# Inverting the chunked recurrence on packed 64x64 blocks instead of full 128x128 matrices

## The chip, the cores and the metric

The kernel runs on one core of one Trainium2 chip. The time is the device time of one execution in microseconds, from the first to the last instruction of the core; the table below gives the median of three runs. One further execution was profiled, and all rows come from that one.

## What is computed

The program computes two transformer blocks on 256 tokens of width 1024. The first has four mixers side by side (a chunked linear recurrence, a spatial gate, a short convolution, a diagonal state-space scan), a merge and a squared-ReLU network; the second has two kinds of attention and a product-key expert layer. Only the recurrence is touched:

```python
def step(state, inp):
    r_t, w_t, k_t, v_t, a_t, b_t = inp
    sa = jnp.einsum('bhij,bhj->bhi', state, a_t)
    state = (state * w_t[:, :, None, :] + sa[..., None] * b_t[:, :, None, :]
             + v_t[..., None] * k_t[:, :, None, :])
    return state, jnp.einsum('bhij,bhj->bhi', state, r_t)
```

It has four heads of 64 channels. The kernel cuts the 256 tokens into two chunks of 128. Within a chunk the steps depend on each other through a strictly triangular 128x128 matrix M for each head (token s acts on token t > s), and the recurrence is solved by multiplying with X = (I - M)^-1, up to the sign that the code folds into M. That is eight inverses of 128x128: four heads, two chunks.

## The kernel before

Weights stream from HBM in units of 128x1024. Each is split into a high and a low part (`unit`, lines 197 to 210): ScalarE makes the high part (204), VectorE and, in the stage looked at here, GpSimd for two of eight slices make the low part (207, 209). TensorE multiplies three times per tile (`mm3`, 227 to 231: high by high, high by low, low by high). Three raw buffers are shared with `ada_steps` (412), whose VectorE steps at 422 and 424 add up the conditioning vectors, with one-column products at 428.

Around this dense stream other parts run as generators (`spawn`, `tick`): `wkv` is the recurrence, `s5_main` the state-space scan, `sg` the spatial gate. Each `yield` gives control back to the dense stream, so the recurrence's steps are laid between the dense products. The framework's scheduler then orders each engine's queue; each queue runs in order. All PSUM tiles of the generators share the name `ax` and six banks.

The inversion is at lines 801 to 836. It doubles the size of the inverted diagonal blocks seven times. Level l takes the part of M that couples neighbouring blocks of 2^l (`mm`, a product with the constant 0/1 mask `lev[:, l]` on GpSimd, 814), and with X the inverse so far and Z its transpose computes `t1 = mm^T Z` (817), copies it to SBUF (`ts`, ScalarE, 823), and adds `ts^T X` to X (830, 836) and `X^T ts` to Z (834, 835). Index n is the chunk; the four heads lie in one tile of 128x4x128 = 512 elements a partition. Level 0 starts from the identity (819, 820), and level 6 needs no new Z. TensorE operands here are full float32. The names `kn`, `s3` hold the masked matrices of the two chunks, `s2`, `s1` their Z, `bt`, `kt` their `ts`; in the rows `s` stands for several of these (numbers are left out).

Line 784 multiplies halves of 64 rows, with the two row halves going to two PSUM tiles. Lines 864 and 865 have 64 output columns, and the two column halves go to one PSUM tile. Lines 1020, 1042 and 1043 are the state-space products on 32 rows or 32 columns.

Of the kernel before, what the change touches and what calls it, by code (L numbers as in the profile page):

```python
# [8 lines left out]
FT = mybir.dt.float32  # L9
# [4 lines left out]
AF = mybir.ActivationFunctionType  # L14
OP = mybir.AluOpType
# [3 lines left out]
P = 128  # L19
# [47 lines left out]
def _constants():  # L67
    f = np.float32
    r = np.arange(P)
    s, t = r[:, None], r[None, :]  # L70
    ident = np.eye(P, dtype=f)
    ones = np.ones((P, P), f)
    bones = ((s // 64) == (t // 64)).astype(f)
    strict = (s < t).astype(f)
    incl = (s <= t).astype(f)
    iota = np.broadcast_to(r.astype(f)[None, :], (P, P))
    rot = np.zeros((P, P), f)
    for h in (0, 64):
        for i in range(8):
            rot[h + i, h + i + 8] = -1.0  # L80
            rot[h + i + 8, h + i] = 1.0
    main = np.concatenate([ident, ones, iota, bones, strict, incl], axis=1)
    lv = []
    for l in range(7):
        b = 1 << l
        lv.append(((s // (2 * b) == t // (2 * b)) & (s % (2 * b) < b) & (t % (2 * b) >= b)).astype(f))
    levels = np.concatenate(lv, axis=1)
    inv = np.power(f(500000.0), -np.arange(8, dtype=f) / f(8)).astype(f)
    ang = (np.arange(S, dtype=f)[:, None] * inv[None, :]).astype(f)
    cos, sin = np.cos(ang).astype(f).T, np.sin(ang).astype(f).T  # L90
    ct, st = np.ones((P, S), f), np.zeros((P, S), f)
    for h in (0, 8, 64, 72):
        ct[h:h + 8], st[h:h + 8] = cos, sin
    tri = np.where(t <= s, f(0), f(-NEG))
    amask = np.concatenate([tri, np.zeros((P, P), f), tri], axis=1)
    sel = np.zeros((P, 8, S), f)
    for h in range(8):
        sel[h::32, h] = 1.0
    att = np.concatenate([rot.T, ct, st, amask, sel.reshape(P, -1)], axis=1).astype(f)
    return main.astype(f), levels.astype(f), att  # L100


def _layout(inputs):
    a = {k: np.asarray(v) for k, v in inputs.items()}
    one = lambda n: a[n][0]
    m = {}
    m["vec"] = _pack_vectors(a)
    m["main"], m["levels"], m["att"] = _constants()
    m["x"] = a["x"].reshape(S, D).T.reshape(8, P, S).transpose(1, 0, 2)
    m["ada"] = one("ada_w").reshape(8, P, 6, D).transpose(2, 0, 1, 3)[2:]  # L110
# [50 lines left out]
class Kernel:  # L161
# [511 lines left out]
    def wkv(self, psum, pw, pA, y):  # L673
        nc, tc = self.nc, self.tc
        V, SC, G, T = nc.vector, nc.scalar, nc.gpsimd, nc.tensor
        def tl(name, shape=(P, 2, S), dt=FT, **kw):
            return pw.tile(list(shape), dt, name=name, **kw)

        lev = tl("lev", [P, 7, P])
        nc.sync.dma_start(lev, self.A["levels"].rearrange("p (a b) -> p a b", a=7))  # L680
        lw = tl("lw", [P, 256])
        nc.sync.dma_start(lw, self.A["lora"])
# [38 lines left out]
        a = tl("s3")  # L721
# [27 lines left out]
        kn = tl("kn")  # L749
# [16 lines left out]
        bt, kt = (tl(n, [P, 4, P]).rearrange("p (c n) t -> p c (n t)", c=2) for n in ("bt", "kt"))  # L766
# [10 lines left out]
        for n in range(2):  # L777
            yield
            for src, dst in ((bt, mb[n]), (kt, mk[n])):
                for par in range(2):  # L780
                    R = slice(64 * par, 64 * par + 64)
# [16 lines left out]
        bk = tl("bk", [P, 2, 2, P])  # L798
        SC.activation(bk, tps, AF.Copy)
        yield  # L800
        X, Z = {}, {}
        idb = self.ident[:, None, :].to_broadcast([P, 4, P])

        def mt4(n):
            return mb[n].rearrange("p a c (x t) -> p (a c) x t", x=2)[:, :, 0, :]

        for n in range(2):
            X[n], Z[n] = tl(f"X{n}", [P, 4, P]), tl(f"s{2 - n}", [P, 4, P])
        for l in range(7):
            mm, t1, ts = {}, {}, {}  # L810
            yield
            for n in range(2):
                mm[n] = tl(("kn", "s3")[n], [P, 4, P])
                G.tensor_tensor(mm[n], mt4(n), lev[:, l:l + 1, :].to_broadcast([P, 4, P]), op=OP.mult)
                t1[n] = psum.tile([P, 4, P], FT, name="ax")
                for h in range(4):
                    T.matmul(t1[n][:, h, :], mm[n][:, h, :], self.ident if l == 0 else Z[n][:, h, :], start=True, stop=True)
                if l == 0:
                    V.tensor_tensor(X[n], mm[n], idb, op=OP.add)
                    V.tensor_tensor(Z[n], t1[n], idb, op=OP.add)  # L820
                else:
                    ts[n] = tl(("bt", "kt")[n], [P, 4, P])
                    SC.activation(ts[n], t1[n], AF.Copy)
            if l == 0:
                continue
            yield
            for n in range(2):
                xp = psum.tile([P, 4, P], FT, name="ax")
                for h in range(4):
                    T.matmul(xp[:, h, :], ts[n][:, h, :], X[n][:, h, :], start=True, stop=True)  # L830
                if l < 6:
                    zps = psum.tile([P, 4, P], FT, name="ax")
                    for h in range(4):
                        T.matmul(zps[:, h, :], X[n][:, h, :], ts[n][:, h, :], start=True, stop=True)
                    V.tensor_tensor(Z[n], Z[n], zps, op=OP.add)
                V.tensor_tensor(X[n], X[n], xp, op=OP.add)
        O = tl("s4", [P, 2, 2, 2, 64])
        st = tl("st", [P, 2, 64])
        for n in range(2):
# [4 lines left out]
            for par in range(2):  # L844
                R = slice(64 * par, 64 * par + 64)
# [13 lines left out]
            if n == 0:  # L859
                sp = psum.tile([P, 2, 64], FT, name="ax")  # L860
                for c in range(2):
                    for par in range(2):
                        R = slice(64 * par, 64 * par + 64)
# [5 lines left out]
            for par in range(2):  # L869
                R = slice(64 * par, 64 * par + 64)  # L870
                op = psum.tile([P, 2, 64], FT, name="ax")
# [24 lines left out]
        of, kq, kn = tl("s3"), tl("s1"), tl("kn")  # L896
# [730 lines left out]
```

## Time and profile before

| what | us |
|---|---|
| median of 3 runs (1606.66 to 1611.36) | 1610.3 |
| the profiled execution | 1612.27 |
| its span | 1610.5 |
| TensorE products busy | 1555.3 |
| VectorE busy | 1141.2 |
| ScalarE busy | 840.0 |
| GpSimd busy | 367.3 |
| mean granted TensorE clock | 0.985 |

PE is TensorE's products, PEld its weight loads, DVE VectorE, ACT ScalarE, POOL GpSimd. Products are pipelined: the time between two starts tells their rate, and the duration of one is longer than that. The clock is told as a share of 2.4 GHz; 0.50 is 1.2 GHz.

### The profile page before, as it was taken

Reading aid. Unit: us, or ns where it says so; the run is one execution under the profiler, and the core shown is the slowest. Engines: PE = TensorE matmul, PEld = TensorE weight load, DVE = VectorE, ACT = ScalarE, POOL = GpSimd, SP = SyncE. Lnnn points to the kernel's source line nnn. Section 1 sums busy time; section 2 is a strip of 40 time slices with the busy share of each in tenths; the row PEclk is TensorE's granted clock in tenths of the full one; section 3 lists DMA queues with packets and bytes.
Section 4 is the critical chain, followed back from the end, with each engine's and each line's share of the span. In section 5 each row is a group of like instructions: output and inputs, shape, how many; then the busy total and the mean of one; then the engine's idle time right before and its main releaser. Section 6 shows DMA issues by size and latency. Waiting matters only on the chain. (4 is left out here: it accounts for less than half of the span.)

```text
span 1610.5 us, 28420 instructions
## 1 busy us (share of the span) xinstructions
PE 1555.3 (97%) x11206; PEld 1444.6 (90%) x11206; DVE 1141.2 (71%) x1800; ACT 840.0 (52%) x1393; POOL 367.3 (23%) x319
## 2 busy tenths in 40 slices
PE   7998999999999989999999999999999999999997
PEld 5897889999999978989999999999999788888886
DVE  7689876688656676557679887888899555555555
ACT  4562223556644445545354547777776445444443
POOL 7516753416500020003784510000000000000000
PEclk9899899999999999999999999999999999999999
DMA  8555446576665643445655565544445666666663
GB/s 333 181 154 156 132 148 191 176 221 223 176 192 177 204 132 118 131 118 165 214 157 176 180 184 149 153 145 145 148 144 155 190 205 185 193 194 195 193 193 125
DMA packets 75446, 279.87 MB, mean 174 GB/s; under 512 B 8368, under 2 KB 8880, under 8 KB 73648
## 3 DMA queue, kind: packets, MB, share of 16 engines
q1 hardware_dynamic: 75312, 278.05, 56.4%
q8 instruction: 88, 1.44, 0.4%
q14 instruction: 46, 0.38, 0.1%
HBM read 275.92 MB, written 2.10 MB: 173 GB/s over the span
## 5 line engine op out<-in xcount | busy, mean ns | idle before, releaser
L204 ACT ACTIVATE whi<-raw 128x1024 fp32r<-128x1024 f32 x453 | 479.0, 1058 | 582.7 <-PE mm L230 240.2
L207 DVE TENSOR_TENSOR wlo<-raw,whi 128x1024 fp32r<-128x1024 f32 (+2 forms) x413 | 501.5, 1216 | 266.5 <-ACT whi L204 265.3
L229 PE MATMUL mm<-hh,whi 128*128 128x256 f32 x1816 | 525.1, 289 | 1.2 <-ACT uD L464 1.2
L231 PE MATMUL mm<-hh,wlo 128*128 128x256 f32 x1816 | 516.8, 285 | 6.0 <-DVE wlo L207 5.2
L230 PE MATMUL mm<-hl,whi 128*128 128x256 f32 x1816 | 513.3, 283 | 1.1 <-DVE hl L1450 0.7
L231 PEld LDWEIGHTS mm<-hh,wlo 128*128 128x128 f32 x1816 | 346.3, 191 | 8.9 <-DVE wlo L207 6.2
L229 PEld LDWEIGHTS mm<-hh,whi 128*128 128x128 f32 x1816 | 345.3, 190 | 9.2 <-issue 7.4
L230 PEld LDWEIGHTS mm<-hl,whi 128*128 128x128 f32 x1816 | 346.5, 191 | 2.9 <-issue 1.4
L209 POOL TENSOR_TENSOR wlo<-raw,whi 128x256 fp32r<-128x256 f32 (+2 forms) x112 | 185.8, 1664 | 138.9 <-ACT whi L204 85.9
L1484 PE MATMUL ax<-whi,ah 128*128 128x512 f32 x512 | 158.7, 391 | 3.9 <-ACT ah L330 3.9
L1484 PE MATMUL ax<-whi,al 128*128 128x512 f32 x512 | 158.5, 391 | 0.0
L1484 PE MATMUL ax<-wlo,ah 128*128 128x512 f32 x512 | 158.0, 390 | 0.0
L1484 PEld LDWEIGHTS ax<-whi,ah 128*128 128x128 f32 x512 | 96.0, 188 | 23.8 <-ACT ah L330 4.1
L1484 PEld LDWEIGHTS ax<-whi,al 128*128 128x128 f32 x512 | 96.5, 189 | 20.5 <-DVE al L331 0.4
L1484 PEld LDWEIGHTS ax<-wlo,ah 128*128 128x128 f32 x512 | 96.4, 188 | 20.1
L1408 ACT ACTIVATE om<-xres,tg 128x128 f32<-128x128 f32 x256 | 84.9, 392 | 1.0 <-DVE xres L1405 1.0
L231 PE MATMUL ax<-hh,wlo 128*128 128x258 f32 x256 | 72.8, 284 | 1.5 <-DVE wlo L207 1.5
L229 PE MATMUL mm<-fh,whi 128*128 128x256 f32 x256 | 73.0, 285 | 0.0
L231 PE MATMUL mm<-fh,wlo 128*128 128x256 f32 x256 | 72.9, 285 | 0.0
L230 PE MATMUL mm<-fl,whi 128*128 128x256 f32 x256 | 72.9, 285 | 0.0
L229 PE MATMUL ax<-hh,whi 128*128 128x258 f32 x256 | 72.7, 284 | 0.0
L230 PE MATMUL ax<-hl,whi 128*128 128x258 f32 x256 | 72.2, 282 | 0.0
(526 smaller groups left out, 2486.1 us busy)
## 6 DMA issues: line engine op xcount, KB each, us to landing
raw<-in_wts SPq DMA_DIRECT2D x453, 512.0 KB, 3.7
raw<-in_ada SPq DMA_DIRECT2D x24, 512.0 KB, 3.8
araw<-in_ada SPq DMA_DIRECT2D x8, 1024.0 KB, 7.9
w0r<-in_w SPq DMA_DIRECT2D x8, 576.0 KB, 8.9
araw<-in_ada SPq DMA_DIRECT2D x8, 512.0 KB, 4.9
x<-in_x SPq DMA_DIRECT2D x1, 1024.0 KB, 5.3
mb<-in_x SPq DMA_DIRECT2D x2, 512.0 KB, 5.5
selh<-in_att SPq DMA_DIRECT2D x1, 1024.0 KB, 7.2
```

The lines of the kernel that those rows point to most:

```text
L204: nc.scalar.activation(hi, raw, AF.Copy)
L207: nc.vector.tensor_tensor(lo[:, :c], raw[:, :c], hi[:, :c].bitcast(FT), op=OP.subtract)
L209: nc.gpsimd.tensor_tensor(lo[:, c:], raw[:, c:], hi[:, c:].bitcast(FT), op=OP.subtract)
L229: mm(ps, wh, xh, start=start, stop=False, **kw)
L230: mm(ps, wh, xl, start=False, stop=False, **kw)
L231: mm(ps, wl, xh, start=False, stop=stop, **kw)
L1408: SC.activation(om[:, j, :], oe[:, j, :], AF.Copy, scale=it["g"][:, t0 + j:t0 + j + 1])
L1484: T.matmul(acc[t][c], a[:, u, z], w[:, c * 512:(c + 1) * 512], start=i + u == 0 and n == 0, stop=i + u == P - 1 and n == 2)
```

## The change

Levels 0 to 5 never couple the two 64-token halves of a chunk. So the change works on the two diagonal 64x64 blocks alone, packed: tokens 0 to 63 on partitions 0 to 63 and tokens 64 to 127 on partitions 64 to 127, with 64 columns each. X, Z, the masked matrices and `t1` then have 256 elements a partition instead of 512, and each product of 128x128 by 128 becomes two of 64x64 by 64, one on the upper row and column half of the array and one on the lower. `mp` is the packed copy of M (four ScalarE copies of 64 partitions), `Xp` the packed X; `lev` holds six masks of 64 columns and an identity. The masks of level l + 1 are issued in front of level l's second step. The last level writes its result into the diagonal blocks of the full X, which GpSimd has filled with zeros before. The seventh level is one coupling: the off-diagonal 64x64 block of M times the two inverses, in two steps, without masks, written to X by ScalarE.

```diff
-    for l in range(7):
+    s6, t6 = s % 64, t[:, :64]
+    for l in range(6):
...
-        lev = tl("lev", [P, 7, P])
+        lev = tl("lev", [P, 7, 64])
...
+        def masked(l):
+            for n in range(2):
+                mm[n] = tl(("kn", "s3")[n], [P, 4, P])[:, 0:2, :].rearrange("p a (b t) -> p (a b) t", b=2)
+                G.tensor_tensor(mm[n], mp[n], lev[:, l:l + 1, :].to_broadcast([P, 4, 64]), op=OP.mult)
+
         for n in range(2):
-            X[n], Z[n] = tl(f"X{n}", [P, 4, P]), tl(f"s{2 - n}", [P, 4, P])
-        for l in range(7):
-            mm, t1, ts = {}, {}, {}
+            X[n] = tl(f"X{n}", [P, 4, P])
+            G.memset(X[n], 0.0)
...
+            for R in halves:
+                SC.activation(mp[n][R], mt4(n)[R, :, R], AF.Copy)
+        masked(0)
+        for l in range(6):
...
-                    T.matmul(t1[n][:, h, :], mm[n][:, h, :], self.ident if l == 0 else Z[n][:, h, :], start=True, stop=True)
+                    for R in halves:
+                        T.matmul(t1[n][R, h, :], mm[n][R, h, :], lev[R, 6, :] if l == 0 else Z[n][R, h, :], start=True, stop=True)
...
+            if l < 5:
+                masked(l + 1)
...
-                    T.matmul(xp[:, h, :], ts[n][:, h, :], X[n][:, h, :], start=True, stop=True)
...
+                    for R in halves:
+                        T.matmul(xp[R, h, :], ts[n][R, h, :], Xp[n][R, h, :], start=True, stop=True)
+                zps = psum.tile([P, 4, 64], FT, name="ax")
+                for h in range(4):
+                    for R in halves:
+                        T.matmul(zps[R, h, :], Xp[n][R, h, :], ts[n][R, h, :], start=True, stop=True)
+                V.tensor_tensor(Z[n], Z[n], zps, op=OP.add)
+                if l < 5:
+                    V.tensor_tensor(Xp[n], Xp[n], xp, op=OP.add)
+                else:
+                    for R in halves:
+                        V.tensor_tensor(X[n][R, :, R], Xp[n][R], xp[R], op=OP.add)
+        yield
+        for n in range(2):
...
+                T.matmul(t1[n][up_, h, :], mt4(n)[lo, h, up_], Z[n][lo, h, :], start=True, stop=True)
...
+            SC.activation(ts[n][up_], t1[n][up_], AF.Copy)
+        yield
+        for n in range(2):
...
+                T.matmul(xp[lo, h, :], ts[n][up_, h, :], X[n][up_, h, up_], start=True, stop=True)
+            SC.activation(X[n][lo, :, up_], xp[lo], AF.Copy)
```

The scheduler lays TensorE's queue as it was: each group of products stands between the same neighbours. On VectorE the order of neighbours shifts in places. This is VectorE's queue at the updates of level 4, before (`acc` is the conditioning sum at 424, `wlo` a low part, `t1`, `t2` and `sc` the state-space scan, `s2` and `s1` the two Z):

```order
L424 SCALAR_TENSOR_TENSOR acc_1963<-raw_2409,ca_106,acc_1963 128x1024
L1030 SCALAR_TENSOR_TENSOR sc_2280<-s5m_82,z_2275 128x256 x2
L1032 TENSOR_TENSOR t1_2283<-sc_2280,s5t_81 128x512
L1033 TENSOR_TENSOR t2_2284<-sc_2280,s5t_81 128x512
L207 TENSOR_TENSOR wlo_2355<-raw_2352,whi_2354 128x768
L207 TENSOR_TENSOR wlo_2416<-raw_2413,whi_2415 128x768
L424 SCALAR_TENSOR_TENSOR acc_1963<-raw_2489,ca_106,acc_1963 128x1024
L835 TENSOR_TENSOR s2_1727<-s2_1727,ax_2390 128x512
L836 TENSOR_TENSOR X0_1726<-X0_1726,ax_2385 128x512
L835 TENSOR_TENSOR s1_1729<-s1_1729,ax_2402 128x512
L836 TENSOR_TENSOR X1_1728<-X1_1728,ax_2397 128x512
```

And the same place of the changed kernel, whose lines 852 and 854 are the two updates, 426 the conditioning sum and 209 the low part:

```order
L1064 SCALAR_TENSOR_TENSOR sc_2374<-s5m_82,z_2369 128x256 x2
L426 SCALAR_TENSOR_TENSOR acc_2009<-raw_2527,ca_106,acc_2009 128x1024
L1066 TENSOR_TENSOR t1_2377<-sc_2374,s5t_81 128x512
L1067 TENSOR_TENSOR t2_2378<-sc_2374,s5t_81 128x512
L209 TENSOR_TENSOR wlo_2457<-raw_2454,whi_2456 128x768
L209 TENSOR_TENSOR wlo_2534<-raw_2531,whi_2533 128x768
L852 TENSOR_TENSOR s2_1730<-s2_1730,ax_2496 128x256
L854 TENSOR_TENSOR Xp0_1728<-Xp0_1728,ax_2487 128x256
L852 TENSOR_TENSOR s1_1737<-s1_1737,ax_2516 128x256
L854 TENSOR_TENSOR Xp1_1735<-Xp1_1735,ax_2507 128x256
L426 SCALAR_TENSOR_TENSOR acc_2009<-raw_2611,ca_106,acc_2009 128x1024
```

The conditioning sum that stood right ahead of the four updates (`raw_2489`, now `raw_2611`) stands behind them. The second place is GpSimd's queue around the masks of level 1, before (`xx` and `z` belong to the state-space scan):

```order
L1035 TENSOR_TENSOR xx_1690<-t1_1686,t2_1687 128x256
L1036 TENSOR_TENSOR xx_1690<-t1_1686,t2_1687 128x256
L209 TENSOR_TENSOR wlo_1751<-raw_1748,whi_1750 128x256
L814 TENSOR_TENSOR kn_1854<-mb0_888,lev_884 128x512
L814 TENSOR_TENSOR s3_1863<-mb1_892,lev_884 128x512
L209 TENSOR_TENSOR wlo_1825<-raw_1822,whi_1824 128x256
L1025 TENSOR_TENSOR z_1804<-t1_1802,t2_1803 128x256
L1026 TENSOR_TENSOR z_1804<-t1_1802,t2_1803 128x256
```

And the same place of the changed kernel:

```order
L1069 TENSOR_TENSOR xx_1690<-t1_1686,t2_1687 128x256
L1070 TENSOR_TENSOR xx_1690<-t1_1686,t2_1687 128x256
L211 TENSOR_TENSOR wlo_1765<-raw_1762,whi_1764 128x256
L814 TENSOR_TENSOR kn_1815<-mp0_1729,lev_884 128x256
L814 TENSOR_TENSOR s3_1817<-mp1_1736,lev_884 128x256
L211 TENSOR_TENSOR wlo_1847<-raw_1844,whi_1846 128x256
L1059 TENSOR_TENSOR z_1826<-t1_1824,t2_1825 128x256
L1060 TENSOR_TENSOR z_1826<-t1_1824,t2_1825 128x256
```

The masks keep their place, though the code issues them earlier; they are half as large and read the packed copy. TensorE's queue at the updates of level 1, before, with the low-part product ahead of it and the state-space products behind:

```order
L231 MATMUL mm_1875<-hh_70,wlo_1751 128x256
L830 MATMUL ax_1907<-X0_1726,bt_1861 128x128 x4
L834 MATMUL ax_1912<-bt_1861,X0_1726 128x128 x4
L830 MATMUL ax_1919<-X1_1728,kt_1870 128x128 x4
L834 MATMUL ax_1924<-kt_1870,X1_1728 128x128 x4
L1042 MATMUL ax_1670<-xx_1690,s5c_80 32x256
```

And now:

```order
L233 MATMUL mm_1905<-hh_70,wlo_1765 128x256
L847 MATMUL ax_1937<-Xp0_1728,bt_1885 64x64 x8
L851 MATMUL ax_1946<-bt_1885,Xp0_1728 64x64 x8
L847 MATMUL ax_1957<-Xp1_1735,kt_1896 64x64 x8
L851 MATMUL ax_1966<-kt_1896,Xp1_1735 64x64 x8
L1076 MATMUL ax_1670<-xx_1690,s5c_80 32x256
```

The neighbours are the same, and each row of four products has become one of eight smaller ones.

## Rows read from the trace of the kernel before

**Rows 1.** The page: engine sums (us, share, instructions), and TensorE's clock in 40 slices.

```profile
PE 1555.3 (97%) x11206; PEld 1444.6 (90%) x11206; DVE 1141.2 (71%) x1800; ACT 840.0 (52%) x1393; POOL 367.3 (23%) x319
...
PEclk9899899999999999999999999999999999999999
```

**Rows 2.** Stretches: busy time of each engine, granted clock, DMA.

```profile
core 0: us, PE busy (x) PEld busy (x) DVE busy (x) ACT busy (x) POOL busy (x), PEclk, DMA share, GB/s
150.00:200.00 50.00, 45.44 (x305) 40.17 (x305) 43.47 (x51) 13.81 (x18) 36.48 (x31) 0.90 0.45 133
200.00:260.00 60.00, 56.48 (x446) 52.81 (x447) 44.71 (x53) 16.71 (x22) 30.86 (x25) 0.97 0.52 159
260.00:300.00 40.00, 39.16 (x313) 37.68 (x312) 22.25 (x30) 17.05 (x34) 16.29 (x14) 0.96 0.66 210
161.20:164.60 3.40, 3.20 (x15) 2.90 (x14) 0.88 (x2) 0.84 (x2) 3.40 (x4) 0.50 0.57 193
174.90:181.60 6.70, 6.70 (x33) 6.70 (x33) 6.08 (x10) 0.16 (x1) 2.67 (x3) 0.50 0.57 164
232.90:236.20 3.30, 3.23 (x12) 2.32 (x12) 2.03 (x3) 1.19 (x2) 2.06 (x2) 0.50 0.29 115
292.40:296.10 3.70, 3.70 (x26) 3.19 (x24) 0.74 (x1) 0.66 (x2) 1.32 (x1) 1.00 0.37 87
```

**Rows 3.** Waits, 140 to 262: who for whom, total us, times, longest.

```profile
ACT whi L204 <- PE mm L230: 44.1, 11, 7.3
...
PE ax L817 <- DVE s L835: 4.2, 2, 3.3
...
PE ax L817 <- POOL kn L814: 3.1, 1, 3.1
```

**Rows 4.** TensorE in order of time (start, us, instruction), level 1 updates.

```profile
167.57 1.05 PE L830 MATMUL ax<-X,bt 128*128 128x128 f32 x8
168.46 1.06 PE L834 MATMUL ax<-bt,X 128*128 128x128 f32 x8
```

**Rows 5.** TensorE in order of time at the column halves.

```profile
268.49 0.28 PE L230 MATMUL mm<-hl,whi 128*128 128x256 f32 x1
268.61 0.28 PE L231 MATMUL mm<-hh,wlo 128*128 128x256 f32 x1
268.82 0.34 PE L864 MATMUL ax<-us,bk 128*64 128x64 f32 x4
268.99 0.29 PE L865 MATMUL ax<-vt,bk 128*64 128x64 f32 x4
269.10 0.33 PE L864 MATMUL ax<-us,bk 128*64 128x64 f32 x4
269.22 0.34 PE L865 MATMUL ax<-vt,bk 128*64 128x64 f32 x4
269.49 0.38 PE L229 MATMUL mm<-yh,whi 128*128 128x256 f32 x1
```

**Rows 6.** TensorE in order of time at the row halves.

```profile
119.25 1.14 PE L784 MATMUL ax<-ar,bt 64*128 64x256 f32 x8
120.22 1.13 PE L784 MATMUL ax<-ar,kt 64*128 64x256 f32 x8
```

**Rows 7.** GpSimd in order of time before the level 1 products.

```profile
158.57 2.29 POOL L814 TENSOR_TENSOR kn<-mb,lev 128x512 f32<-128x512 f32 x1
160.82 2.09 POOL L814 TENSOR_TENSOR s<-mb,lev 128x512 f32<-128x512 f32 x1
```

**Rows 8.** VectorE in order of time at the level 4 updates.

```profile
229.79 1.28 DVE L424 SCALAR_TENSOR_TENSOR acc<-raw,ca,acc 128x1024 f32<-128x1024 f32 x1 [2.95 <-DMA raw<-in_ada]
230.99 0.68 DVE L835 TENSOR_TENSOR s<-s,ax 128x512 f32<-128x512 f32 x1
```

**Rows 9.** TensorE in order of time behind the level 1 updates.

```profile
173.69 2.56 PE L428 MATMUL ax<-main,acc 128*128 128x1 f32 x16 [0.35 <-DVE s L835]
```

**Rows 10.** VectorE groups, 140 to 262: count, busy us, mean ns, idle before.

```profile
L835 DVE TENSOR_TENSOR s<-s,ax 128x512 f32<-128x512 f32 x10 | 6.8, 678 | 1.7 <-PE ax L834 1.7
...
L430 DVE TENSOR_TENSOR mod<-ax,vec 128x8 f32<-128x8 f32 x2 | 0.3, 162 | 0.4 <-PE ax L428 0.4
```

More of the change, by code (lines that the diff above doesn't have):

```diff
@@ L83, in _constants @@
     lv = []
-    for l in range(7):
+    s6, t6 = s % 64, t[:, :64]
+    for l in range(6):
         b = 1 << l
-        lv.append(((s // (2 * b) == t // (2 * b)) & (s % (2 * b) < b) & (t % (2 * b) >= b)).astype(f))
+        lv.append(((s6 // (2 * b) == t6 // (2 * b)) & (s6 % (2 * b) < b) & (t6 % (2 * b) >= b)).astype(f))
+    lv.append((s6 == t6).astype(f))
     levels = np.concatenate(lv, axis=1)
@@ L800, in wkv @@
         yield
-        X, Z = {}, {}
-        idb = self.ident[:, None, :].to_broadcast([P, 4, P])
+        X, Xp, Z, mp, mm = {}, {}, {}, {}, {}
+        idp = lev[:, 6:7, :].to_broadcast([P, 4, 64])
+        lo, up_ = slice(0, 64), slice(64, 128)
+        halves = (lo, up_)
         def mt4(n):
             return mb[n].rearrange("p a c (x t) -> p (a c) x t", x=2)[:, :, 0, :]
+        def masked(l):
+            for n in range(2):
+                mm[n] = tl(("kn", "s3")[n], [P, 4, P])[:, 0:2, :].rearrange("p a (b t) -> p (a b) t", b=2)
+                G.tensor_tensor(mm[n], mp[n], lev[:, l:l + 1, :].to_broadcast([P, 4, 64]), op=OP.mult)
@@ L807, in wkv @@
         for n in range(2):
-            X[n], Z[n] = tl(f"X{n}", [P, 4, P]), tl(f"s{2 - n}", [P, 4, P])
-        for l in range(7):
-            mm, t1, ts = {}, {}, {}
+            X[n] = tl(f"X{n}", [P, 4, P])
+            G.memset(X[n], 0.0)
+            Xp[n], mp[n] = tl(f"Xp{n}", [P, 4, 64]), tl(f"mp{n}", [P, 4, 64])
+            Z[n] = tl(f"s{2 - n}", [P, 4, P])[:, 0:2, :].rearrange("p a (b t) -> p (a b) t", b=2)
+            for R in halves:
+                SC.activation(mp[n][R], mt4(n)[R, :, R], AF.Copy)
@@ L811, in wkv @@
+        masked(0)
+        for l in range(6):
+            t1, ts = {}, {}
             yield
             for n in range(2):
-                mm[n] = tl(("kn", "s3")[n], [P, 4, P])
-                G.tensor_tensor(mm[n], mt4(n), lev[:, l:l + 1, :].to_broadcast([P, 4, P]), op=OP.mult)
-                t1[n] = psum.tile([P, 4, P], FT, name="ax")
+                t1[n] = psum.tile([P, 4, 64], FT, name="ax")
                 for h in range(4):
-                    T.matmul(t1[n][:, h, :], mm[n][:, h, :], self.ident if l == 0 else Z[n][:, h, :], start=True, stop=True)
+                    for R in halves:
+                        T.matmul(t1[n][R, h, :], mm[n][R, h, :], lev[R, 6, :] if l == 0 else Z[n][R, h, :], start=True, stop=True)
@@ L818, in wkv @@
                 if l == 0:
-                    V.tensor_tensor(X[n], mm[n], idb, op=OP.add)
-                    V.tensor_tensor(Z[n], t1[n], idb, op=OP.add)
+                    V.tensor_tensor(Xp[n], mm[n], idp, op=OP.add)
+                    V.tensor_tensor(Z[n], t1[n], idp, op=OP.add)
                 else:
-                    ts[n] = tl(("bt", "kt")[n], [P, 4, P])
+                    ts[n] = tl(("bt", "kt")[n], [P, 4, P])[:, 0:2, :].rearrange("p a (b t) -> p (a b) t", b=2)
                     SC.activation(ts[n], t1[n], AF.Copy)
+            if l < 5:
+                masked(l + 1)
@@ L827, in wkv @@
             for n in range(2):
-                xp = psum.tile([P, 4, P], FT, name="ax")
+                xp = psum.tile([P, 4, 64], FT, name="ax")
                 for h in range(4):
-                    T.matmul(xp[:, h, :], ts[n][:, h, :], X[n][:, h, :], start=True, stop=True)
[L831 to L836, printed above, removed]
+                    for R in halves:
[12 more added lines that the diff above has]
+        for n in range(2):
+            t1[n] = psum.tile([P, 4, 64], FT, name="ax")
+            for h in range(4):
+                T.matmul(t1[n][up_, h, :], mt4(n)[lo, h, up_], Z[n][lo, h, :], start=True, stop=True)
+            ts[n] = tl(("bt", "kt")[n], [P, 4, P])[:, 0:2, :].rearrange("p a (b t) -> p (a b) t", b=2)
+            SC.activation(ts[n][up_], t1[n][up_], AF.Copy)
+        yield
+        for n in range(2):
+            xp = psum.tile([P, 4, 64], FT, name="ax")
+            for h in range(4):
+                T.matmul(xp[lo, h, :], ts[n][up_, h, :], X[n][up_, h, up_], start=True, stop=True)
+            SC.activation(X[n][lo, :, up_], xp[lo], AF.Copy)
         O = tl("s4", [P, 2, 2, 2, 64])
```

## The prediction

> **What bounds the kernel now.** I read the engine sums first, then the stretches, the waits, and the single instructions of the stage. TensorE is busy for 97% of the span, and its clock row shows full speed almost everywhere [rows 1]. So time saved on TensorE shortens the program unless something else takes its place. The stage that is changed lies between 150 and 256 us. There TensorE is less full: 45.44 of 50 us up to 200, 56.48 of 60 after it, against 39.16 of 40 in the stretch that follows, and VectorE is nearly as full, 43.47 of 50 [rows 2]. In the waits of that stage ScalarE waits 44.1 us for TensorE to free a weight buffer, which is the mark of a bound TensorE; TensorE itself waits 4.2 us for the updated `Z` from VectorE and 3.1 us for a masked matrix from GpSimd [rows 3]. Three stretches of the stage ran at 0.50, which is 1.2 instead of 2.4 GHz: 3.4, 6.8 and 3.4 us long, of which rows stand for 161.2, 174.9 and 232.9 [rows 2]. The first and third follow the two long waits.
>
> The profiled execution took 1612.3 us with a span of 1610.5; the median of the runs shown is 1610.3. I make the sum against 1612.3 and take 2.0 off at the end.
>
> **TensorE, removed.** The inversion issues 144 products of 128x128 by 128 columns, 56 at line 817, 48 at 830 and 40 at 834. Each four-head call of four products shows as x8, so a float32 product is two instructions, 288 in all. Eight begin 0.89 us apart [rows 4], 0.111 us each at full clock: 288 x 0.111 = 32.0 us.
>
> **TensorE, added.** Levels 0 to 5 now take 96 products for `t1` and 160 for the two updates, the coupling 16: 272 products of 64x64 by 64 columns, 544 instructions. No row of before has this tile. The nearest is line 864/865, 128 rows, 64 output columns, 64 moving columns, where the two column halves are separate tiles. There four instructions begin each 0.11 to 0.12 us, 0.029 us each, and the whole group of 16, from the dense neighbour at 268.61 to the next at 269.49, costs 0.88 us less that neighbour's own step of 0.12 (268.49 to 268.61), so 0.76. 16 x 0.029 is 0.46; the other 0.30 is what going to another tile shape and back costs [rows 5]. Line 784 shows the same for two row halves: eight instructions of 256 columns begin in 0.97 us, 0.121 each, hardly more than the 0.111 that one of 128 columns takes on the whole array, so two halves must be running side by side [rows 4, 6]. Of the new tiles one takes the first 64 rows and the first 64 columns of the array, the other the last 64 of both, so they differ in rows and in columns, and they alternate in the code. I take the column row: 512 instructions of the levels x 0.029 = 14.8 us. The 32 of the coupling all sit on one tile, which goes at twice that, 0.057: 1.8 us. There are 13 groups (six `t1`, five updates, two of the coupling) that change shape, 13 x 0.30 = 3.9. Sum 20.5, a gain of 11.5 us. The bounds: by TensorE's queue seven of the groups are followed by state-space products, which change shape anyway, so the price could be 7 x 0.15 = 1 us less; if the two tiles never overlap it is 544 x 0.057 + 3.9 = 34.9 us, 2.9 more than before.
>
> On this the Trainium skill has a rule that speaks against the change: in "TensorEngine Tiling (Array Packing)", Restrictions and Gotchas, Gotcha 1, it says that row tiles write to different PSUM banks and can't use one bank at the same time. Line 784 does keep its row halves in two PSUM tiles, and the new code puts both row halves into one. By that rule the 34.9 would hold, and it is a rival below. Line 864 writes both halves of one PSUM tile side by side, but with the same rows; no row here has different rows in one bank. I put little on it, since the halves of the new tiles go to different output partitions.
>
> **The waits.** The 3.1 us wait ends when GpSimd finishes the mask of level 1, 158.57 to 160.86 [rows 7]. In the program the masks are now issued a level ahead, but in GpSimd's queue they stand where they stood, behind the same low-part subtraction. What shrinks is the mask, from 512 to 256 elements a partition: 2.29 us becomes 1.15 by its own rate, so 1.1 us of the wait goes and 2 stay. The longest of the waits for `Z`, 3.3 us, is different. VectorE stood for 2.95 us at an `acc` step whose weights came late, with the four updates queued behind it until 229.79 + 1.28, and TensorE wanted the first `Z` [rows 8]. In the new order the four updates of that level stand ahead of that `acc`, so I count all 3.3. With it should go the half clock at 232.9, which costs half of its 3.3 us, 1.6. Sum 6.0 us. What is late next is VectorE. The half clock at 174.9 follows one-column products of line 428 that stay [rows 9], and I leave it.
>
> **VectorE, ScalarE, GpSimd.** 26 operations of 0.678 us (lines 819, 820, 835, 836) become 28 of 256 elements. The row at 8 elements is 0.162 and at 512 0.678 [rows 10]; the line between gives 0.416: 17.6 becomes 11.6, 6.0 us less. ScalarE's copies halve in size and four small ones are added, about even, and it is idle most of this stage [rows 2]. GpSimd loses two masks and half of the rest, and gains two fills of 512 elements that fall where it has nothing else; nothing there is on the path but the level-1 mask. The mask table's load is half as large and early.
>
> Between 150 and 200 TensorE would shed 14.2 - 9.2 = 5.0 us of products (128 instructions become 256, six groups) and 1.1 of waiting, VectorE 12 x 0.262 = 3.1. VectorE had 6.5 us to spare there, in pieces. I let the difference, 3 us, come back as new waits on VectorE.
>
> Sum: 11.5 + 6.0 - 3 = 14.5 us. 1612.3 - 14.5 - 2.0 = **1596 us**.
>
> **Rivals.**
> 1. VectorE sets the pace of the whole stage. For it: 87% busy from 150 to 200, and TensorE's waits there name it. Against it: 75% after 200, and the 44.1 us that ScalarE waits for TensorE. Then only VectorE's own 6.0 us are gained: 1604.
> 2. The two tiles take turns (the rule on banks). 34.9 instead of 32.0, with the waits still gone: 1612.3 + 2.9 - 6.0 - 2.0 = 1607. Rows 5 and 6 speak against it, each for one half of the case.
> 3. The clock falls. The new groups use half of the array, and each could be followed by a stretch at 1.2 GHz like that at 161.2, where 15 instructions took 3.4 us, 1.7 lost. All 13 would cost 22 us: 1612.3 - 14.5 + 22 - 2.0 = 1618, slower. It decides from nine such stretches on, where it eats the 14.5, and shows as slower than the measurement's bound from twelve. Against it: line 784's stretch and the 3.7 us at 292.4 of thin 64-column products, with changes of shape in it, kept 1.00 [rows 2].
>
> **Chances.** Forecast 0.71, with its own range of 1588 to 1601 (below if the 2 us of wait and the clock at 161 go too, above if VectorE takes back 8 rather than 3); VectorE's pace 0.16; taking turns 0.09; the clock 0.04. About 0.3%, 5 us, is what can be told from no change. Faster by more holds the forecast and two thirds of the first rival: 0.82. Within it: the rest of that and the second: 0.14. Slower: the third, 0.04. The range that leaves out no more than 2 in 10 is 1587 to 1606.
>
> **What would show it.** In the new profile a group of 32 `t1` instructions should last 1.2 us and one of 64 about 2.1, with starts on the two tiles close together; 0.057 between all of them means taking turns. The wait at 228 should be gone and that for the level-1 mask be near 2. New waits should name VectorE (the low parts or `Z`). Fewer stretches at 0.50 between 150 and 260, not more. The stretch after 260 should be as before, 15 us earlier. The prediction is wrong if TensorE's idle time in this stage grows by as much as its products shrink.

## The result, and the profile after

The changed kernel took 1588.9 us (median of four runs, 1585.9 to 1591.4), the kernel before 1608.5 beside it. The ratio is 0.988, with an interval of 0.986 to 0.990. In two later comparisons the ratio was 0.989 both times (intervals 0.988 to 0.991 and 0.987 to 0.991). So the change gives 18 to 20 us. The forecast was 14.5 on 1610.3, to 1596, with a range of 1587 to 1606 and a chance of 0.82 for faster.

The profiled execution took 1588.85 us with a span of 1587.1. These are its engine sums and its clock row, to be held against [rows 1]:

```profile
PE 1533.5 (97%) x11462; PEld 1423.3 (90%) x11462; DVE 1134.1 (71%) x1800; ACT 839.8 (53%) x1399; POOL 358.7 (23%) x319
...
PEclk9899899999999999999999999999999999999999
```

TensorE is 21.8 us less busy, though it has 256 instructions more, and VectorE is 7.1 us less busy. The stretches of the stage follow, with the columns of [rows 2]; the two short ones are those of this stage that ran at 0.50:

```profile
150.00:200.00 50.00, 45.23 (x505) 39.48 (x504) 43.04 (x56) 14.08 (x20) 35.48 (x33) 0.90 0.49 159
200.00:260.00 60.00, 58.70 (x628) 54.93 (x629) 46.71 (x58) 21.71 (x38) 32.45 (x26) 1.00 0.65 210
158.10:161.40 3.30, 3.30 (x17) 3.30 (x17) 2.30 (x3) 0.57 (x1) 3.30 (x5) 0.50 0.89 349
168.40:175.10 6.70, 6.70 (x34) 6.48 (x36) 6.07 (x9) 0.12 (x1) 1.99 (x3) 0.50 0.52 161
```

After 200 us TensorE is full (58.70 of 60, before 56.48). Before 200 it is not (45.23 of 50, before 45.44). One update of level 3 on TensorE, in order of time (start, duration, engine, line, tiles, instructions), where before such a group was eight by eight [rows 4]:

```profile
196.83 0.68 PE L847 MATMUL ax<-Xp,bt 64*64 64x64 f32 x16
197.35 0.63 PE L851 MATMUL ax<-bt,Xp 64*64 64x64 f32 x16
197.81 0.63 PE L847 MATMUL ax<-Xp,kt 64*64 64x64 f32 x16
198.28 0.63 PE L851 MATMUL ax<-kt,Xp 64*64 64x64 f32 x16
198.84 0.62 PE L1076 MATMUL ax<-xx,s5c 128*32 128x256 f32 x2
```

The second and third begin 0.46 us apart for 16 instructions, 0.029 each. The whole group takes 2.01 us. A `t1` group, here that of level 4, takes 1.08 up to the next instruction:

```profile
203.92 0.68 PE L831 MATMUL ax<-s,kn 64*64 64x64 f32 x16
204.43 0.63 PE L831 MATMUL ax<-s,s 64*64 64x64 f32 x16
205.00 0.62 PE L1076 MATMUL ax<-xx,s5c 128*32 128x256 f32 x2
```

And VectorE's queue at the updates of level 4, which answers to [rows 8]:

```profile
212.48 2.36 DVE L209 TENSOR_TENSOR wlo<-raw,whi 128x768 fp32r<-128x768 f32 x2
214.76 0.41 DVE L852 TENSOR_TENSOR s<-s,ax 128x256 f32<-128x256 f32 x1
215.09 0.41 DVE L854 TENSOR_TENSOR Xp<-Xp,ax 128x256 f32<-128x256 f32 x1
215.42 0.41 DVE L852 TENSOR_TENSOR s<-s,ax 128x256 f32<-128x256 f32 x1
215.75 0.41 DVE L854 TENSOR_TENSOR Xp<-Xp,ax 128x256 f32<-128x256 f32 x1
217.13 1.28 DVE L426 SCALAR_TENSOR_TENSOR acc<-raw,ca,acc 128x1024 f32<-128x1024 f32 x1 [0.97 <-DMA raw<-in_ada]
```

The conditioning sum still waits 0.97 us for its load, but behind the updates. TensorE no longer waits for a Z there. What TensorE waits for between 127 and 240 us, against [rows 3], which begins at 140 (between 127 and 140 the kernel before has one more wait, 2.7 us for a low part at 137.3):

```profile
PE ax L831 <- POOL kn L814: 2.5, 1, 2.5
PE mm L231 <- ACT gate L581: 1.9, 1, 1.9
PE mm L233 <- DVE wlo L209: 1.9, 2, 1.7
...
PE ax L831 <- POOL xx L1069: 1.2, 1, 1.2
PE ax L430 <- DVE s L852: 0.8, 1, 0.8
```

To compare executions I cut the stage at two dense products that both kernels have, the 193rd and the 337th at line 229 (231 after) of those that take `hh`, at 127.2 and 260.7 us before. From the instructions between them I take TensorE's idle time, and half of the time that it worked at 0.50. What is left is work at full clock.

| stage, us | total | idle | half of the time at 0.50 | rest |
|---|---|---|---|---|
| before | 133.5 | 10.8 | 8.4 | 114.3 |
| after | 115.1 | 8.5 | 5.1 | 101.5 |
| after, second profile | 114.8 | 11.1 | 1.7 | 102.0 |
| after, third profile | 114.4 | 8.5 | 5.0 | 101.0 |

The stage gives 18.4 us, of which 12.8 are work and 5.6 waits and clock (18.7 and 19.1 us in the other two profiles). Of the kernel before there is this one profile. Behind it the two traces part by another 2.0 us, and in the other two profiles by 1.2 and 0.5. The remaining 3.0 us of the profiled pair arise before anything of the change runs: the 65th such product is at 64.5 us before and at 61.5 after.

### The profile page after: what moved, and what is told of

Its sections match the earlier page's. It is cut to its first block, busy times and chain, and to the rows that moved or that the text cites. A ratio compares the mean times of both kernels' runs of the same rounds, so it can differ in the third digit from the quotient of the medians.

```text
span 1587.1 us, 28930 instructions
## 1 busy us (share of the span) xinstructions
PE 1533.5 (97%) x11462; PEld 1423.3 (90%) x11462; DVE 1134.1 (71%) x1800; ACT 839.8 (53%) x1399; POOL 358.7 (23%) x319
## 3 DMA queue, kind: packets, MB, share of 16 engines
q8 instruction: 90, 1.47, 0.4%
## 5 line engine op out<-in xcount | busy, mean ns | idle before, releaser
L1518 PEld LDWEIGHTS ax<-whi,al 128*128 128x128 f32 x512 | 96.5, 189 | 20.5 <-DVE al L333 0.4
```

What stands on the lines that cost most here:

```text
L1518: T.matmul(acc[t][c], a[:, u, z], w[:, c * 512:(c + 1) * 512], start=i + u == 0 and n == 0, stop=i + u == P - 1 and n == 2)
```

## The experiments

**Every product of levels 0 to 5 issued twice.**

```diff
-                    for R in halves:
+                    for R in halves * 2:
...
```

> The changed kernel with every 64x64 product of levels 0 to 5 issued twice (512 more instructions, nothing else). Theory: TensorE sets the pace of the stage and the products' time is what the change gained; a pair of tiles costs 0.029 us an instruction, so 512 x 0.029 = 14.8 us come on top: 1604, and groups of 64 become 128 instructions in 3.9 us. Rival (VectorE sets the pace, products are half hidden): at most 5 us more, 1594, with waits on VectorE shrinking instead.

1606.5 us, ratio 0.998 (0.997 to 1.000). The edit stands at all three products. The rest in the stage rose from 101.5 to 117.1, 15.6 for 512 instructions, 0.030 each, and the stage as a whole from 115.1 to 129.4, so shorter waits and less half clock took up only 1.3 of it. The same update of level 3:

```profile
200.51 1.15 PE L847 MATMUL ax<-Xp,bt 64*64 64x64 f32 x32
201.49 1.10 PE L851 MATMUL ax<-bt,Xp 64*64 64x64 f32 x32
202.42 1.10 PE L847 MATMUL ax<-Xp,kt 64*64 64x64 f32 x32
203.35 1.10 PE L851 MATMUL ax<-kt,Xp 64*64 64x64 f32 x32
```

So TensorE's products are on the path almost in full, and VectorE's pace as the bound of the whole stage falls.

**The two halves one after the other.** All four heads of the upper half, then of the lower.

```diff
-                for h in range(4):
-                    for R in halves:
+                for R in halves:
+                    for h in range(4):
...
```

> The changed kernel with the four heads of the upper half issued first and then the four of the lower half, instead of in turns. Theory A (each tile has a stream of its own, as the row halves of line 784, whose two products of one half also follow each other): groups of 64 stay at 2.0 us, 1589 within 2. Rival B (only neighbours in the order overlap): about 0.06 us an instruction, groups of 64 at 3.5 to 3.9 us, 1589 + 12 = 1601.

1595.6 us, ratio 0.993 (0.990 to 0.996). A `t1` group takes 1.47 us (1.08 in turns), an update group 2.62 (2.01), and the rest in the stage rose by 5.0. Both theories miss. This is the beginning of an update group:

```profile
196.75 0.79 PE L847 MATMUL ax<-Xp,bt 64*64 64x64 f32 x13
197.32 0.27 PE L851 MATMUL ax<-bt,Xp 64*64 64x64 f32 x1
197.38 0.22 PE L847 MATMUL ax<-Xp,bt 64*64 64x64 f32 x1
197.43 0.22 PE L851 MATMUL ax<-bt,Xp 64*64 64x64 f32 x1
197.43 0.22 PE L847 MATMUL ax<-Xp,bt 64*64 64x64 f32 x1
```

Where a run of eight on one half meets a run on the other, the last few of the one and the first few of the other begin in turns; inside a run they begin 0.058 us apart. What is lost is about a third of the overlap, not all of it (taking turns throughout would be 64 x 0.061 = 3.9 us a group).

**Before, with the conditioning sum behind the updates of level 4.** One added order on VectorE, the only row that moves:

```diff
+                if part == 3 and k == 7:
+                    ins = [i for i in nc.cur_bb.bb.instructions[n:] if i.engine == PIN[0]][-1]
+                    self.tc.add_manual_dep(ins, self.upd.name, ..., reason="issue order")
```

> The kernel before, with one edit: the last conditioning step of part 3 is tied behind the four updates of level 4 on VectorE, as the changed kernel's queue has it. Theory: that order alone ends the 3.3 us wait at 228.5 and with it the half clock at 232.9 (1.6): 1608.5 - 5 = 1603.5, no wait over 0.5 us ahead of the level 5 products. Rival (the weights that came late only hold up the next thing): the wait comes back at a low part or at the next conditioning step, 1607 to 1609.

1604.1 us, ratio 0.998 (0.996 to 0.999), 5.0 less than before. The sum waits 1.94 us for its load, behind the updates, and `t1` of level 5 begins without a wait:

```profile
225.80 0.67 DVE L841 TENSOR_TENSOR X<-X,ax 128x512 f32<-128x512 f32 x1
228.41 1.28 DVE L425 SCALAR_TENSOR_TENSOR acc<-raw,ca,acc 128x1024 f32<-128x1024 f32 x1 [1.94 <-DMA raw<-in_ada]
...
226.73 1.05 PE L822 MATMUL ax<-s,kn 128*128 128x128 f32 x8
```

So about 5 us (1 to 6 by the interval) can be had in the old kernel by the order of one row on VectorE, without small matrices. That the same 5 are part of the change's 20 is likely and not shown: the changed kernel with that row ahead of the updates was not run, and there the sum waits 0.97 us for its load, not 2.95. In the one profile the stage gives 4.1 us, 1.8 of idle time and 2.2 of clock: the 3.3 us wait is gone, while ahead of the moved row, where all queues are the same, the waits are 1.6 us longer than in the profile before.

**Masks two levels ahead.** The changed kernel, with the two masked matrices of a level in alternate halves of the tiles `kn` and `s3`. Only GpSimd's queue changes.

```diff
-            if l < 5:
-                masked(l + 1)
+            if l < 4:
+                masked(l + 2)
...
```

> The changed kernel with the masked matrices in two buffers and issued two levels ahead, so that the level 1 mask stands early in GpSimd's queue. Theory: the 2.5 us wait for it goes, and with it the half clock right behind (1.7): 1589 - 4 = 1585. Rival 1 (VectorE's Z of level 0 is late too): the wait is put down to VectorE and shrinks by less than 1 us, 1588 to 1589. Rival 2 (the clock falls all the same): 1586.5, with 0.50 still near 158.

1593.1 us, ratio 0.990 (0.988 to 0.992): nothing gained, and all three forecasts lay lower. The 2.5 us for the mask are gone, and others stand in their place (idle time in the stage 11.0 us, in the three profiles of the changed kernel 8.5 to 11.1):

```profile
PE ax L430 <- DVE s L855: 2.1, 1, 2.1
PE ax L850 <- ACT kt L840: 1.7, 1, 1.7
PE ax L834 <- DVE s L855: 1.2, 1, 1.2
PE ax L834 <- DVE s L837: 1.0, 1, 1.0
```

**The changed kernel again, and the masks two ahead with the conditioning sum tied behind the second Z of level 0.** At that Z the first of the new waits had begun. The tie is of the same form as above (part 2, seventh step).

> The changed kernel once more, as the measure for the other run of this call. If the start-up accounts for the part of the difference that stands ahead of the stage, the gain within the stage (from the dense tile before it to the one behind it, against the profile of before) is again 18.4 us within 1, whatever the start-up is: ratio 0.987 to 0.990, 1588 to 1593. If the waits in the stage are chance, the stage's gain should differ by more than 2 us.

> The masks two levels ahead, and the conditioning sum (part 2, seventh step) that stood on VectorE between the two Z of level 0 tied behind the second. The scheduler moves more rows with it: a yl and some low parts between 157 and 190 us change places with conditioning sums. Theory A (the waits that came back with the masks two ahead start at that sum: 0.98 us at the Z, and from it 1.7 at the copy kt and 1.3 of the 2.1 ahead of the one-column products): these go, and with the mask wait gone as well the kernel is 2 to 4 us faster than the changed one. Theory B (VectorE has a fixed amount to do between 150 and 190 us and TensorE has to wait for some of it, whatever the order): the waits turn up at another name (low part or yl), and the time is within 1.5 us of the changed kernel.

1590.6 us (0.989, 0.988 to 0.991) and 1589.9 us (0.988, 0.987 to 0.990): the same, so theory A falls. In the first the stage gives 18.7 us, within 1 of 18.4 as expected. The small waits are gone in the tied version but for 0.5 us, and one stands in their place, with a long stretch at 0.50 that begins within it (an instruction on TensorE, then the stretch):

```profile
169.68 3.57 PE L435 MATMUL ax<-main,acc 128*128 128x1 f32 x16 [3.84 <-DVE s L861]
...
167.40:177.50 10.10, 7.82 (x36) 7.82 (x37) 8.63 (x14) 1.06 (x1) 5.72 (x6) 0.50 0.56 169
```

**The one-column products a tick later.** These 16 instructions wait for the PSUM tile of a Z update; here they stand behind the first step of level 2, the only group that moves on TensorE. Once in the changed kernel, once with the masks two ahead as well, and the changed kernel beside them.

```diff
+            if part == 3 and k == 0:
+                self.ada_end(psum, 2, self.late)
+        if part == 2:
+            self.late = acc
+        else:
+            self.ada_end(psum, part, acc)
...
```

> The changed kernel with the sixteen one-column products of conditioning part 2 one tick later: on TensorE's queue that group alone moves, from behind the updates of level 1 to behind the first step of level 2; the other engines shift a few rows. Theory A (the group waits for a PSUM tile of a Z update, 0.85 us in one profile and 2.3 in the other, and that wait brings on the half clock behind it, 6.8 and 3.4 us long): wait and half clock go, 2.5 to 4.5 us less than the changed kernel run in this call. Theory B (sixteen products of one column are what the clock answers to, with or without a wait): a stretch of 3.4 to 6.8 us at 0.50 follows the group at its new place, and only the wait of 0.8 to 2.3 us is gained; if VectorE is late there as well, nothing.

> The same move on top of the masks two levels ahead. If both long waits of the stage are gone and nothing returns: the mask wait 2.5 us, its half clock 1.7, and the 2.5 to 4.5 of the one-column products, together 6 to 8 us less than the changed kernel, about 1582. If VectorE's low parts and Z updates are what TensorE waits for in the end (as with the masks alone, where 0.98 and 1.68 us came back and the sum was nothing), within 2 us of the changed kernel.

> The changed kernel, as the measure for the two others of this call: ratio to before 0.987 to 0.991.

1588.3 us (0.987, 0.985 to 0.990), 1590.1 (0.989, 0.987 to 0.991), and 1590.0 for the changed kernel (0.989, 0.987 to 0.991): the same again. The wait is at `t1` of level 3 now, here in the second:

```profile
185.35 0.93 PE L843 MATMUL ax<-s,kn 64*64 64x64 f32 x16 [3.51 <-DVE s L864]
```

The group itself waits for nothing at its new place. In the first version a stretch at 0.50 of 3.4 us stands behind its beginning all the same (at 173.1, the group at 171.6); in the second there is none there. So neither theory holds for the clock in both.

**Less for VectorE.** In the seven profiles so far of the changed kernel and of its versions with masks or one-column products moved, the first update of Z at level 2 began 60 to 63 us after the stage's first mark. So VectorE's amount of work was the next suspect. Most of four conditioning sums is left out here, and the scheduler moves some rows with it.

```diff
+                w = slice(0, 8) if part == 2 and k > 4 or part == 3 and k == 1 else slice(0, D)
-                nc.vector.scalar_tensor_tensor(acc, raw, ...)
+                nc.vector.scalar_tensor_tensor(acc[:, w], raw[:, w], ...)
```

> The changed kernel with four conditioning steps on VectorE (part 2, sixth to eighth, and part 3, second) over 8 instead of 1024 columns, so that most of these sums is left out: VectorE has about 4 x 1.15 = 4.6 us less to do between 150 and 190 us, TensorE's queue stays, and some low parts move up. Theory V (VectorE sets the pace up to level 3: in six profiles, whatever was done to the masks and to the one-column products, the first Z of level 2 was finished 60 to 63 us after the same dense product, and before it TensorE waits now here, now there): that Z comes 3 to 4 us sooner, and the kernel is 3 to 5 us faster than the changed one, 1584 to 1587, part of it only if the level-1 mask still waits for GpSimd. Theory W (GpSimd's steps or the loads set the pace, VectorE only hands on): the Z stays within 1 us, and so does the time.

> The same four steps thin, with the masks two levels ahead and the one-column products a tick later, so that neither GpSimd's mask nor the PSUM tile of the one-column products holds TensorE up. Theory V: all of VectorE's 4.6 us comes out, with the 2 to 3 us that the two moves had won by level 2 and given back at level 3: 5 to 7 us less than the changed kernel, 1582 to 1585. Theory W: 1588 to 1592.

1589.3 us (0.988, 0.985 to 0.990) and 1589.8 (0.989, 0.987 to 0.990): theory V falls on the time. In the first version the first Z of level 1 came 2.9 us sooner (39.6 us behind the mark), but that of level 2 began at 61.7 us, as ever. In the second it began at 59.5, and the stage was the shortest of all (111.8, with 7.3 idle), but 1.5 to 3 us were lost again behind it, where a wait of 1.5 us for `yl` and two stretches at 0.50 stand between 247 and 263 us.

**Fewer loads.** ScalarE waits for weight loads 39.8 us in the stage, before 27.1. So the last suspect was the loads into the three shared buffers. The slices of eight loads are left out of the conditioning here, and rows move in all four queues.

```diff
+            if part == 2 and k or part == 3 and k == 1:
+                nc.vector.scalar_tensor_tensor(acc, acc, self.ca[:, k:k + 1], acc, ...)
+                yield
+                continue
```

> The changed kernel without eight of the conditioning loads (part 2, second to eighth step, and part 3, second): VectorE's eight steps stay, of the same size, but add the running sum to itself, so these slices of the conditioning are left out. The three raw buffers then serve the dense weights alone between 125 and 175 us. Theory R (the loads are what the stage waits for in the end: ScalarE waits 39.8 us for weight loads between 127 and 240 against 27.1 before, and 49.0 and 56.9 in the two versions without the mask's wait): ScalarE's wait for loads falls below 20 us, TensorE's idle time in the stage from 8.5 to 5 or less, with fewer half clocks: 3 to 6 us faster than the changed kernel, 1584 to 1587. Rival (the chain of the state space over TensorE, VectorE and GpSimd, and VectorE's queue, hold it): ScalarE's wait changes its name only, and the time is within 1.5 us of the changed kernel, 1588.5 to 1591.5.

1591.7 us, ratio 0.990 (0.989 to 0.992). ScalarE's wait for loads fell as theory R has it. TensorE's idle time fell from 8.5 us only to 7.5, not to 5, and its time at 0.50 rose to 17.1:

```profile
ACT whi L206 <- DMA raw<-in_wts: 14.4, 5, 7.3
...
PE ax L835 <- POOL kn L818: 1.7, 1, 1.7
PE ax L835 <- POOL s L818: 1.7, 1, 1.7
```

Theory R falls too. Over all versions of the changed kernel that keep its products and their order, the rest in the stage was 100.5 to 102.0 us, and idle time and clock together 12.5 to 15.4, but for the one with 10.7. What keeps that sum up is not settled. It is neither GpSimd's masks, nor the place of the one-column products, nor four of VectorE's sums, nor the loads, each taken alone. The hand-over of the state-space steps between TensorE, VectorE and GpSimd was not tested, and the traces point there: in all ten of these profiles VectorE waits 0.6 to 0.7 us for GpSimd's `z` shortly ahead of the first Z of level 2, and in nine also 0.6 to 2.0 us for its `xx`, as here in the changed kernel:

```profile
180.58 0.69 DVE L1057 TENSOR_TENSOR t<-ax,s5t 128x512 f32<-128x512 f32 x1 [2.02 <-POOL xx L1070]
```

The tenth is the version with the shortest stage.

## Why the prediction was right, and where its sizes were off

**The products**: right. Six groups of 1.08, five of 2.01 and two of 1.07 us, waits left out, and 13 x 0.09 on the way in (the first instruction begins 0.21 us after the last dense one, where dense ones are 0.12 apart) are 19.8 us, as against 20.5 in the sum: a gain of 12.2 rather than 11.5. Two tiles in turns take 0.029 to 0.030 us an instruction and one tile alone 0.061 (forecast 0.029 and 0.057), and a change of shape and back costs 0.21 us (forecast 0.30). The doubled products show that almost all of it is on the path. The rest in the stage fell by 12.8; what the other 0.6 are was not broken down.

**The 3.3 us at `t1` of level 5 and the half clock behind it**: right, by the order on VectorE, as the third experiment shows in the kernel before (5.0 us for the pair, 4.9 in the sum; that they agree so well is in part luck, since the interval is 1 to 6).

**The level-1 mask**: the step was right, its size and one reading were off. 2.5 us of waiting remain, not 2. The two masks took 0.72 us each, less than half of the 2.29 and 2.09 of before [rows 7], but the low part ahead of them took 1.70, where it had taken 0.72. GpSimd's rows, and the conditioning sum that VectorE ran at that time, first before, then after:

```profile
157.88 0.72 POOL L209 TENSOR_TENSOR wlo<-raw,whi 128x256 fp32r<-128x256 f32 x1
158.45 1.27 DVE L424 SCALAR_TENSOR_TENSOR acc<-raw,ca,acc 128x1024 f32<-128x1024 f32 x1
...
153.54 1.42 DVE L426 SCALAR_TENSOR_TENSOR acc<-raw,ca,acc 128x1024 f32<-128x1024 f32 x1
153.84 1.70 POOL L211 TENSOR_TENSOR wlo<-raw,whi 128x256 fp32r<-128x256 f32 x1
155.51 0.72 POOL L814 TENSOR_TENSOR kn<-mp,lev 128x256 f32<-128x256 f32 x1
156.19 0.72 POOL L814 TENSOR_TENSOR s<-mp,lev 128x256 f32<-128x256 f32 x1
```

The 2.29 us were not the mask's own rate, as the forecast took them to be: the mask began 0.12 us behind the sum, and six of the fourteen masks of before took 1.27 to 1.30. After the change the sum stands a row earlier, between the two Z of level 0, and it is the low part that begins just behind it, 0.30 us. It took 1.70 or 1.71 in all seven profiles with these two rows side by side, and 0.72 in both with the old order. So what the mask lost went in part to the row ahead of it. That the sum holds GpSimd up is read from these rows; no run tests it by itself.

**The 3 us that were to come back as waits on VectorE**: this is the term that was mis-sized. The idle time fell by 2.3 us. With 3.3 gone at level 5 and 0.6 at the mask, 1.6 came back: at `gate` and the low parts, at the one-column products and at level 3. And the clock gave more than was counted: the time at 0.50 fell from 17.1 to 10.2 us, worth 3.3, where the sum had 1.6. So 3.0 us for waits and clock became 5.6. Part of that is chance: the half clock at 137.3, which the forecast had not looked at, is not there in this profile, but the third profile of the same kernel has one at 132.6, and the second has just one stretch in the stage and more idle time for it. Idle time and clock together are 12.8 to 13.6 us in the three, against 19.2 in the one profile before.

**VectorE's own work**: the count was off by two. It is 26 operations after as before, not 28, and they took 11.2 us instead of 17.6, 6.4 less where the forecast had 6.0. Only the first rival's 1604 rests on it.

**The base.** 2.0 us were taken off for the profiled execution of before. Its difference to the medians of these comparisons (1608.1 to 1608.5) is 4, so 1596 stood 2 us too high from the start.

**The rivals.** That the two tiles take turns falls: 0.029 us, not 0.061, in one PSUM tile. On this the Trainium skill says in "TensorEngine Tiling (Array Packing)", Restrictions and Gotchas, Gotcha 1, that different row tiles can't use the same PSUM bank at the same time. The rows of this case do not agree: here two row tiles that write different partitions of one PSUM tile begin 0.029 us apart. That the clock falls after each of the groups falls as well: with 13 groups there are one to three stretches at 0.50 in the stage in three profiles, and four in the one before. VectorE's pace was wrong as a bound for the whole stage. Waits that come back wherever one is taken away are what six runs met up to level 3; that VectorE's amount of work is their reason is not shown, since with four sums left out of it the time stayed.

## What to carry to other kernels

A block-diagonal product of two 64x64 blocks is worth packing onto two corners of the array, with the two tiles in turns instruction by instruction: 0.029 us an instruction instead of 0.061, and two of them stand for one of 0.111 on the whole array. Beside it a change of tile shape and back costs about 0.2 us a group. Ahead of a stretch with many hand-overs, count a wait as gained only where what ends it next is known: here one reordered row gave 5 us, and four versions that took away waits of 0.9 to 2.5 us gave nothing.

## What was not expected of the hardware

The start of the program varies by up to 7 us between executions, and it is mostly the clock. The stretch at 0.50 near 40 us was 13.7 us long in the profile before, 10.2 in that after and 3.4 in its second profile:

```profile
41.80:55.30 13.50, 11.93 (x59) 9.84 (x59) 7.83 (x5) 5.15 (x10) 13.27 (x6) 0.50 0.55 223
...
38.70:48.70 10.00, 9.25 (x50) 7.49 (x49) 4.96 (x5) 4.56 (x8) 9.92 (x7) 0.50 0.68 273
...
39.70:43.00 3.30, 3.04 (x22) 1.95 (x22) 0.81 (x1) 1.27 (x2) 3.30 (x5) 0.50 1.00 393
```

The 65th dense product followed at 64.5, 61.5 and 57.5 us. The order of every queue up to there is the same in all three. Half of TensorE's busy time in the stretch explains 1.3 of the first 3.0 us and 4.4 of the whole 7.0. Besides, in the first profile dense products begin 0.21 us apart up to 24.7 us, where in the other two they are 0.12 apart from 20 us on. So the difference of two single profiles is read between marks inside the stage, not from their ends. And the time of one row on GpSimd does not vary by chance here as it seems to at first: the low part ahead of the level-1 masks took 0.72 us with the one order on VectorE and 1.70 with the other, as told above, and the twelve masks of the changed kernel took 0.72 to 1.72 in one execution, the two longest where a conditioning sum had begun on VectorE 0.6 us ahead of them; where the sum began 0.16 us behind the mask, it took 0.72.
